# Gates of A and B, output projection and seven eighths of the up projection as seven products of halves of tokens, contraction and columns

## The chip, the cores and the metric

The kernel runs on one core of a Trainium2 chip. A core has a matrix engine (TensorE, PE in the profile; PEld is its weight loading), a vector engine (VectorE, DVE), a scalar engine (ScalarE, ACT), a general engine (GpSimd, POOL) and a queue engine (SyncE, SP) that issues transfers. The metric is the device time in microseconds. Three runs of the kernel before took 857.31, 858.68 and 859.06 us; the median is 858.68.

## The reference, cut to what matters

One encoder layer is applied to two groups of 256 tokens (512 in all) with shared weights, in float32.

```python
h = rms_norm(x, norm1_g)
proj = h @ w_in
qa, ka, va, qb, kb, vb, qm, ga, gb, gm = jnp.split(proj, ...)
...
merged = (jax.nn.sigmoid(ga) * (oa.reshape(B_, S, W_A) @ w_branch_a)
          + jax.nn.sigmoid(gb) * (ob.reshape(B_, S, W_B_OUT) @ w_branch_b)
          + jax.nn.sigmoid(gm) * (om.reshape(B_, S, W_M) @ w_branch_m))
x = x + merged @ w_out
h2 = rms_norm(x, norm2_g)
x = x + jnp.square(jax.nn.relu(h2 @ w_up)) @ w_down
...
return rms_norm(x, final_norm_g)
```

The model width is 1024 and the MLP's inner width 4096. Branch A is a windowed attention (512 channels out), B a dilated one (256), M a cross-attention to a memory (512).

## The kernel before

**Arithmetic.** Every float32 factor is split into a high half, rounded to the type that PE takes in one pass, and a low half, the rest. A product is three matmuls (`mm3`, lines 193 to 197): high by high, high by low, low by high. So each weight tile of 128 x 1024 numbers costs a load, a copy on ACT (high) and a subtraction on DVE or POOL (low): `halves` and `chunk`, lines 158 to 167. Two raw tiles and ten split tiles (five chunks) are there for weights.

**Layout.** Activations stand channels on partitions and tokens along the free dimension, eight tiles of 128 channels and 512 tokens. `fm` (line 199) makes one tile of 128 output channels and all 512 tokens from eight weight blocks of 128 x 128: 8 x 3 = 24 matmuls of 512 columns.

**Order.** The program is a list of units (`unit`, `run`, lines 145 to 191). `run` fetches and splits the weights of units ahead of the one that it emits; `ahead` says how many weight tiles (3 in the stages of this change). Everything on PE, DVE and ACT goes through `InOrder` (lines 62 to 74) and is executed in just this order by each engine; POOL's and SP's instructions are placed by the scheduler. What follows a product (reading its bank) is put on the list `later` and emitted with `flush` one unit on; the low halves of some weights and forms stand on the list `lows` and are emitted at the next unit.

**Stages.** Memory keys and values, projections and attention run to about 321 us. Then, for each of eight tiles of 128 output channels (`ff`), come a gate A and a gate B product (`gate`, line 764: 24 matmuls each) and `branches` (line 771: 12 for A, 6 for B, 12 for M), whose results are gated on DVE and summed on POOL; the gate of M was made before, between the attentions (`P_gm`). `merge` (line 791) splits the sums. `out_proj` (line 811) makes eight output channels tiles, adds x and splits the result with the second norm's gain (`H`). Last is the MLP in eight groups of 512 inner channels (line 1067): the up products of group c (`up`, four tiles in two halves each) alternate with the down products of group c-1. The down projection of groups 0 to 6 is already done as seven products of halves: `parts` (line 912) loads four blocks of the weight and makes their sums with accumulating transfers on POOL, `form` (line 931) makes sums of the activations on DVE, `product` (line 970) the matmuls, 512 columns each. The last group goes through `last_down` (line 1019).

Of the kernel before, what the change touches and what calls it, by code (L numbers as in the profile page):

```python
# [10 lines left out]
F32 = mybir.dt.float32  # L11
# [5 lines left out]
P = 128  # L17
# [60 lines left out]
def encoder_kernel(ctx: ExitStack, tc: tile.TileContext, a: dict, out: bass.AP):  # L78
# [32 lines left out]
    def f(x):  # L111
        return x.bitcast(F32)
# [34 lines left out]
    def unit(fn, *srcs):  # L147
        units.append((fn, srcs))
# [44 lines left out]
    def mm3(o, wh, wl, xh, xl, first, last, more=False):  # L193

        E.matmul(o, wh, xh, start=first, stop=False, skip_group_check=more)
        E.matmul(o, wh, xl, start=False, stop=False, skip_group_check=more)
        E.matmul(o, wl, xh, start=False, stop=last, skip_group_check=more)

    def fm(w, X, o):

        n = len(X)
        for k in range(n):
            c = slice(k * P, (k + 1) * P)
            mm3(o, w[0][:, c], w[1][:, c], X[k][:, 0], X[k][:, 1], k == 0, k == n - 1)
# [554 lines left out]
        unit(flush)  # L759


    MG, wb, sg = [], [], {}

    def gate(w, ff, br):
        p = bank()
        fm(w, X, p)
        g = h2("g")
        A.activation(g, p, AF.Sigmoid)
        sg[ff, br] = g

    def branches(w, *more):
        ff = len(MG)
        if more:
            wb[:] = more
        A.activation(GM[ff], GM[ff], AF.Sigmoid)
        sg[ff, 2] = GM[ff]
        c0 = (ff % 4) * 256
        parts = ((w[0][:, :512], w[1][:, :512], OA), (wb[0][0][:, c0:c0 + 256], wb[0][1][:, c0:c0 + 256], OB),
                 (w[0][:, 512:], w[1][:, 512:], OM))
        for br, (wh, wl, O) in enumerate(parts):  # L780
            p = bank()
            fm((wh, wl), O, p)
            V.tensor_tensor(sg[ff, br], p, sg[ff, br], op=ALU.mult)
        eng = V if ff == KD - 1 else G
        eng.tensor_tensor(sg[ff, 0], sg[ff, 0], sg[ff, 1], op=ALU.add)
        eng.tensor_tensor(sg[ff, 0], sg[ff, 0], sg[ff, 2], op=ALU.add)
        MG.append(sg[ff, 0])

    M = []

    def merge(*ks):
        for k in ks:
            x = s4("mg")
            A.activation(x[:, 0], MG[k], AF.Copy)
            (V, G)[k % 2 if k < KD - 1 else 0].tensor_tensor(x[:, 1], MG[k], f(x[:, 0]), op=ALU.subtract)
# [10 lines left out]
    unit(lambda: merge(KD - 1))  # L806


    X1, H = [], []

    def out_proj(w):
        ff = len(H)
        r = h2("xr")
        A.dma_start(r, a["xT"][:, ff])
        p = bank()
        fm(w, M, p)
        V.tensor_tensor(r, p, r, op=ALU.add)
        X1.append(r)
        x = s4("h")
        A.activation(x[:, 0], r, AF.Copy, scale=gains[:, 2, ff:ff + 1])  # L820
        V.scalar_tensor_tensor(x[:, 1], r, gains[:, 2, ff:ff + 1], f(x[:, 0]), op0=ALU.mult,
                               op1=ALU.subtract)
        H.append(x)

    for ff in range(KD):
        unit(out_proj, (a["w_o"][ff],))

# [14 lines left out]
    def mlp_pool():  # L842
        stages.close()
        at[0] = stages.enter_context(tc.tile_pool(name="ml", bufs=1))

    def block_tile():
        return at[0].tile([P, 1024], F32, tag="blk", name=nm("blk"), bufs=8)

    def turn_x1(t, hh):

# [20 lines left out]
    def up(w, ff, half):  # L871

        if half == 0:
            up_bank[ff] = w, bank()
        w, p = up_bank[ff]
        for k in range(4 * half, 4 * half + 4):
            c = slice(k * P, (k + 1) * P)
            mm3(p, w[0][:, c], w[1][:, c], H[k][:, 0], H[k][:, 1], k == 0, k == KD - 1)
        flush(9)
        if half:  # L880
            later.append(lambda: put_up(ff, p))
# [20 lines left out]
    def load_blocks(c):  # L902

        if c in blocks:
            return
        t = {n: block_tile() for n in "T2BC"}
        for n, b in (("T", "11"), ("2", "21"), ("C", "12"), ("B", "22")):
            SP.dma_start(t[n], block(c, b))
        G.dma_start(t["C"], block(c, "22"), accum_op=ALU.add)
        blocks[c] = t  # L910

    def parts(c, n):

        def go():
            load_blocks(c)
            hi, lo = w_tile(), w_tile()
            src = blocks[c][n[0]]
            A.activation(hi, src, AF.Copy)

            def low():  # L920
                V.tensor_tensor(lo, src, f(hi), op=ALU.subtract)
                if n[1:]:
                    G.dma_start(src, block(c, n[1:]), accum_op=ALU.add)  # L923

            lows.append(low)
            return hi, lo
        return go
# [3 lines left out]
    def form(c, name):  # L931

        lo, hi = UP[c, 0], UP[c, 1]
        A11, A21, A12, A22 = lo[:, :, :S], lo[:, :, S:], hi[:, :, :S], hi[:, :, S:]

        def less(u, v):
            d = h2("f").rearrange("p (j t) -> p j t", j=2)
            V.tensor_tensor(d, u, v, op=ALU.subtract)
            return d

        if name in ("P1", "P2", "Q4"):
            src = {"P1": A11, "P2": A12, "Q4": A22}[name]
        elif name == "Q5":
            src = forms[c, "S1"] = less(A21, A22)
        elif name == "Q6":
            src = forms[c, "S2"] = less(A11, forms.pop((c, "S1")))
        elif name == "P7":
            src = less(A11, A21)
        else:
            src = less(A12, forms.pop((c, "S2")))  # L950
# [8 lines left out]
    def add_to(k, i, p, op=ALU.add):  # L959
        if (k, i) in acc:  # L960
            V.tensor_tensor(acc[k, i], acc[k, i], p, op=op)
        else:
# [1 line left out]
            A.activation(acc[k, i], p, AF.Copy, scale=1.0 if op == ALU.add else -1.0)  # L964


    PRODUCTS = dict(P1=("T12", "a", "V", -1), P2=("2", "a", "11", 1), Q5=("T22", "d", "G", 1),
                    Q6=("T21", "c", "V", 1), P7=("C", "e", "G", -1), Q3=("B", "d", "12", 1), Q4=("T", "e", "21", 1))

    def product(w, c, name):  # L970
        _, bk, to, sign = PRODUCTS[name]
# [86 lines left out]
    unit(mlp_pool)  # L1058
    ORDER = ("P1", "P2", "Q5", "Q6", "P7", "Q3", "Q4")


    SUMMED = {1: ("12", "12"), 2: ("11", "11"), 3: ("21", "21"), 4: ("12", "V"), 5: ("21", "V", 1), 6: ("22", "G")}

    def make(c, n):
        unit(lambda: form(c, ORDER[n]))

    for c in range(NC):
        for h in range(8):
            ff, half = 4 * c + h // 2, h % 2
            unit(lambda *w, ff=ff, half=half: up(w[0] if w else None, ff, half), *([(a["w_up"][ff],)] if half == 0 else []))  # L1070
            if c == 0:
                unit(lambda h=h: turn_x1(h % 4, h // 4))
            if h == 1 and c < NC - 1:
                unit(lambda c=c: load_blocks(c))
            if h == 7 and c == NC - 2:
                unit(fetch_x1)
            if c == NC - 1 and h == 6:
                unit(lambda: ahead.__setitem__(0, 2))
            if c == NC - 1 and h in SUMMED:
                unit(lambda n=SUMMED[h]: later.append(lambda: combine(*n)))  # L1080
            if c and h < 7:
                for n in ((1, 2) if h == 0 else (h + 2,)):
                    if n < 7:
                        make(c - 1, n)
                unit(lambda w, c=c - 1, n=ORDER[h]: product(w, c, n), (parts(c - 1, PRODUCTS[ORDER[h]][0]),))
        if c == 0:
            unit(inv_ms)
            unit(lambda: ahead.__setitem__(0, 3))
        if c < NC - 1:
            make(c, 0)  # L1090
    unit(lambda *w: (kept.update({(0, 0): w[0], (1, 0): w[1]}), last_down(0, (0, 1))),
         *[(block(NC - 1, n),) for n in ("11", "21")])
    unit(lambda: later.append(lambda: combine("22", "V")))
# [84 lines left out]
```

## Time and profile before

| | |
|---|---|
| time, median of 3 runs | 858.68 us (857.31 to 859.06) |
| profiled execution | 859.08 us |
| its span, first to last instruction | 857.3 us |
| PE busy | 844.4 us (99%), 4080 matmuls |
| weight loads busy | 703.8 us (82%) |
| DVE busy | 462.8 us (54%) |
| ACT busy | 397.1 us (46%) |
| POOL busy | 216.0 us (25%) |
| read from memory | 101.93 MB |
| mean clock of PE granted | 0.993 |

The span is cut into 40 slices of 21.4 us on the page; a digit is the tenths of a slice in which an engine was busy. The groups of the page name an instruction by what it writes and reads: `ps<-x,w` is a product of normed activations and a weight, `ps<-mg,w` one of the output projection, `ps<-h,w` an up product, `ps<-w,f` a down product, `w<-raw,w` the low half of a weight, `f` a form, `acc` a sum of down products.

### The profile page before, as it was taken

Reading aid. Unit: us, or ns where it says so; the run is one execution under the profiler, and the core shown is the slowest. Engines: PE = TensorE matmul, PEld = TensorE weight load, DVE = VectorE, ACT = ScalarE, POOL = GpSimd, SP = SyncE. Lnnn points to the kernel's source line nnn. Section 1 sums busy time; section 2 is a strip of 40 time slices with the busy share of each in tenths; the row PEclk is TensorE's granted clock in tenths of the full one; section 3 lists DMA queues with packets and bytes.
Section 4 is the critical chain, followed back from the end, with each engine's and each line's share of the span. In section 5 each row is a group of like instructions: output and inputs, shape, how many; then the busy total and the mean of one; then the engine's idle time right before and its main releaser. Section 6 shows DMA issues by size and latency. Waiting matters only on the chain.

```text
span 857.3 us, 10785 instructions
## 1 busy us (share of the span) xinstructions
PE 844.4 (99%) x4080; PEld 703.8 (82%) x4080; DVE 462.8 (54%) x737; ACT 397.1 (46%) x690; POOL 216.0 (25%) x161
## 2 busy tenths in 40 slices
PE   9999999999999999999999999999999999999996
PEld 7788998888888888888888788888888888888885
DVE  6575535465452311423435542465767666767895
ACT  6455545565554333222323227564445353545453
POOL 2314554656556543211123000000000000000001
PEclk9999999999999999999999999999999999999998
DMA  8343122324241228432322445374747465645322
GB/s 284 115 119 109 62 99 86 98 63 115 85 119 64 75 74 286 132 99 86 110 99 74 147 147 161 110 204 107 205 109 208 111 185 121 178 120 172 75 75 98
DMA packets 47468, 106.87 MB, mean 125 GB/s; under 512 B 19358, under 2 KB 19604, under 8 KB 47416
## 3 DMA queue, kind: packets, MB, share of 16 engines
q1 hardware_dynamic: 39992, 85.69, 30.2%
q0 software_dynamic: 4256, 14.73, 9.7%
q10 hardware_dynamic: 3168, 5.77, 2.0%
q8 instruction: 32, 0.52, 0.3%
q14 instruction: 20, 0.16, 0.1%
HBM read 101.93 MB, written 4.24 MB: 124 GB/s over the span
## 4 chain that ended last, share of the span: by engine, by line
PE 84%; DVE 8%; ACT 5%; issue 2%; DMA 1%; POOL 0%; POOLq 0%; SPq 0%; DVEq 0%; ACTq 0%
PE ps L72 77%; PE sc L72 3%; PE o L72 2%; DVE w L72 2%; PE tp L72 2%; ACT w L72 2%; DVE f L72 1%; ACT sp L72 1%; DVE sp L72 1%; DMA mr<-in_memT 1%; ACT f L72 1%; DVE sq L72 0%; ACT r L72 0%; DVE mg L72 0%; DVE acc L72 0%
## 5 line engine op out<-in xcount | busy, mean ns | idle before, releaser
L72 PE MATMUL ps<-x,w 128*128 128x512 f32 x1080 | 252.5, 391 | 0.0
L72 PEld LDWEIGHTS ps<-x,w 128*128 128x128 f32 x1080 | 201.0, 188 | 41.3
L72 PE MATMUL ps<-h,w 128*128 128x512 f32 x768 | 184.5, 391 | 0.0
L72 PEld LDWEIGHTS ps<-h,w 128*128 128x128 f32 x768 | 143.7, 188 | 29.5
L72 PE MATMUL ps<-w,f 128*128 128x512 f32 (+1 forms) x696 | 164.1, 387 | 1.3 <-DVE acc L72 1.0
L72 DVE TENSOR_TENSOR w<-raw,w 128x1024 fp32r<-128x1024 f32 (+1 forms) x79 | 96.4, 1223 | 115.3 <-ACT w L72 115.2
L72 PEld LDWEIGHTS ps<-w,f 128*128 128x128 f32 x696 | 128.7, 188 | 29.9 <-issue 3.4
L72 ACT ACTIVATE w<-raw 128x1024 fp32r<-128x1024 f32 (+2 forms) x116 | 119.7, 1036 | 21.9 <-DMA raw<-in_w_mem 7.5
L161 POOL TENSOR_TENSOR w<-raw,w 128x1024 fp32r<-128x1024 f32 (+1 forms) x37 | 87.3, 2361 | 120.1 <-ACT w L72 94.9
L72 DVE TENSOR_TENSOR w<-blk,w 128x1024 fp32r<-128x1024 f32 x49 | 59.5, 1224 | 47.7 <-ACT w L72 47.6
L923 POOL DMA_DIRECT2D blk<-in_w_dn x21 | 18.1, 864 | 240.2 <-DVE w L72 240.2
L72 ACT ACTIVATE w<-blk 128x1024 fp32r<-128x1024 f32 x49 | 50.7, 1047 | 15.4 <-DMA blk<-in_w_dn 15.4
L72 DVE TENSOR_TENSOR acc<-acc,ps 128x512 f32<-128x512 f32 x82 | 52.9, 682 | 2.9 <-PE ps L72 2.9
L72 ACT ACTIVATE f<-f 128x512 fp32r<-128x512 f32 x28 | 17.7, 633 | 75.4 <-DVE f L72 75.4
L72 ACT ACTIVATE sp<-sp,st 128x256 f32<-128x256 f32 (+1 forms) x48 | 25.8, 538 | 57.7 <-DVE st L72 57.7
L72 ACT ACTIVATE g<-ps 128x512 f32<-128x512 f32 x16 | 9.6, 598 | 88.4 <-PE ps L72 88.4
L72 DVE TENSOR_TENSOR sum<-o,lo 64x256 f32<-64x256 f32 x24 | 10.0, 417 | 66.5 <-ACT lo L72 66.3
L72 PE MATMUL ps<-mg,w 128*128 128x512 f32 x192 | 44.2, 391 | 1.5 <-ACT mg L72 0.9
L72 PEld LDWEIGHTS ps<-mg,w 128*128 128x128 f32 x192 | 36.0, 188 | 9.6 <-ACT mg L72 1.3
L72 ACT ACTIVATE r<-ps 128x512 f32<-128x512 f32 x32 | 18.9, 591 | 50.7 <-PE ps L72 50.7
L72 PE MATMUL ps<-w,x 128*128 128x384 f32 (+1 forms) x192 | 39.9, 363 | 0.0
L469 POOL TENSOR_TENSOR sp<-sp,st 128x512 f32<-128x512 f32 (+1 forms) x32 | 36.7, 1147 | 6.5 <-DVE st L72 3.6
(146 smaller groups left out, 959.2 us busy)
## 6 DMA issues: line engine op xcount, KB each, us to landing
raw<-in_w_up SPq DMA_DIRECT2D x32, 512.0 KB, 4.7
blk<-in_w_dn SPq DMA_DIRECT2D x28, 512.0 KB, 6.7
blk<-in_w_dn POOLq DMA_DIRECT2D x28, 512.0 KB, 5.7
raw<-in_w_g SPq DMA_DIRECT2D x24, 512.0 KB, 3.3
raw<-in_w_b SPq DMA_DIRECT2D x12, 512.0 KB, 3.3
raw<-in_w_bam SPq DMA_DIRECT2D x8, 512.0 KB, 3.3
raw<-in_w_o SPq DMA_DIRECT2D x8, 512.0 KB, 3.2
raw<-in_w_mem SPq DMA_DIRECT2D x7, 512.0 KB, 3.3
```

What stands on the lines that cost most here:

```text
L72: return self.tc.keep_in_program_order(method(*args, **kw))
L161: sub[0].tensor_tensor(lo[:, c], raw[:, c], f(hi[:, c]), op=ALU.subtract)
L469: G.tensor_tensor(s[:, :, :w], s[:, :, :w], st[:, 6:8].unsqueeze(2).to_broadcast([P, 2, w]), op=ALU.mult)
L923: G.dma_start(src, block(c, n[1:]), accum_op=ALU.add)
```

## The change

The gates of A and B, the output projection and the up projection of groups 1 to 7 are made as seven products of halves. A group is 512 output channels; tokens, contraction and output channels are halved, which gives four blocks of activations (512 contraction channels x 256 tokens), four of weights and four of results (256 channels x 256 tokens).

- `halves_of` makes the sums of the activations' blocks once for a stage, in eight pieces: S1 (pieces 0, 1; the form of Q5), S2 (2, 3; Q6), S4 (4, 5; Q3) and S3 (6, 7; P7, written over the second half of the first four tiles). Each ends with a high half on ACT and a low half on DVE.
- `seven` makes the products in the order P1, P2, Q5, Q3, Q6, P7, Q4. A product is 24 matmuls of 256 columns in one bank. Its weights stand in two tiles: T (block 11, to which an accumulating transfer of POOL adds 12, 22 and 21 after the splits of P1, Q5 and Q6) and C (12 and 22); two more come raw. Each product has one 128 x 1024 split on ACT and DVE. `take` reads the banks: two copies on ACT and one read in place, and five operations of DVE a group.
- Gates: two halves of the channels (q) and two branches alternate. The branch M products (`memory_branch`) move ahead of all gates, with one piece of the forms after each; A and B (`branches`) follow each q. Their gating and sums are all on DVE now, by halves of the tokens.
- Output projection: two groups alternate, with a piece of M's forms after each of the first eight products. `put` adds x and splits H by quarters of 256 tokens.
- Up: group 0 stays as it was, with another order of the contraction and six pieces of H's forms beside it. Groups 1 to 7 alternate a product of `up_seven` with a down product. The down products come in the same new order (Q3 before Q6), and their blocks 21 and 22 come through the raw tiles.

On DVE, the output projection before, where a result tile `xr` follows the product `ps` and is split into `h`, with one weight `w` to split between two of them:

```order
L72 TENSOR_TENSOR xr_4075<-ps_4077,xr_4075 128x512
L72 SCALAR_TENSOR_TENSOR h_4103<-xr_4075,gains,h_4103 128x512
L72 TENSOR_TENSOR w_4108<-raw_4106,w_4107 128x1024
L72 TENSOR_TENSOR xr_4112<-ps_4114,xr_4112 128x512
L72 SCALAR_TENSOR_TENSOR h_4140<-xr_4112,gains,h_4140 128x512
L72 TENSOR_TENSOR w_4145<-raw_4143,w_4144 128x1024
```

and on DVE in the changed program, between the weights of the products Q3 of the two groups (`w_4805`, `w_4851`) and with the form that these read (`f_4635` its high half, `f_4636` its low half):

```order
L72 TENSOR_TENSOR w_4805<-raw_4806,w_4804 128x1024
L72 TENSOR_TENSOR d_4810<-mg_4499,d_4725 128x256
L72 TENSOR_TENSOR d_4810<-d_4810,mg_4499 128x256
L72 TENSOR_TENSOR d_4810<-mg_4502,d_4725 128x256
L72 TENSOR_TENSOR d_4810<-d_4810,mg_4502 128x256
L72 TENSOR_TENSOR f_4634<-d_4810,f_4633 128x512
L72 TENSOR_TENSOR xr_4645<-ps_4693,xr_4645 128x256
L72 SCALAR_TENSOR_TENSOR h_4842<-xr_4645,gains,h_4842 128x256
L72 TENSOR_TENSOR xr_4647<-ps_4693,xr_4647 128x256
L72 SCALAR_TENSOR_TENSOR h_4846<-xr_4647,gains,h_4846 128x256
L72 TENSOR_TENSOR w_4851<-raw_4852,w_4850 128x1024
L72 TENSOR_TENSOR d_4856<-mg_4581,d_4765 128x256
```

Where one tile of 512 columns and its split stood between two weights, a piece of the forms and four operations on quarters stand now.

At the start of the gate stage, DVE in the changed program takes the first memory product (`ps_3172`, gated in place in `q_2700`), the weight of the fifth memory product (`w_3217`), the second piece of X's forms and the next memory product:

```order
L72 TENSOR_TENSOR f_3156<-d_3191,f_3155 128x512
L72 TENSOR_TENSOR q_2700<-ps_3172,q_2700 128x512
L72 TENSOR_TENSOR w_3217<-raw_3215,w_3216 128x512
L72 TENSOR_TENSOR d_3222<-x_462,x_514 128x512
L72 TENSOR_TENSOR d_3221<-d_3222 128x256
L72 TENSOR_TENSOR d_3225<-x_466,x_517 128x512
L72 TENSOR_TENSOR d_3221<-d_3225 128x256
L72 TENSOR_TENSOR f_3156<-d_3221,f_3155 128x512
L72 TENSOR_TENSOR q_2782<-ps_3201,q_2782 128x512
```

Before, DVE had at this place only the low halves of the gates' weights and the multiplies of the three branches; all rows of `d` and `f` are new.

On POOL in an MLP group of the changed program, the accumulating transfers into C of the next down and up group (`blk_6450`, `blk_6572`) stand ahead of the first ones into T of this group (`blk_6161`, `blk_6039`):

```order
L861 DMA blk_5747<-in_w_up 128x2x512
L1136 DMA blk_5609<-in_w_dn 128x1024
L1118 DMA blk_6450<-in_w_dn 128x1024
L847 DMA blk_6572<-in_w_up 128x2x512
L861 DMA blk_6161<-in_w_up 128x2x512
L1136 DMA blk_6039<-in_w_dn 128x1024
```

Before, POOL had four such transfers a group, one into C and three into T, all of the down projection.

The core of the diff:

```diff
+    SEVEN = ("P1", "P2", "Q5", "Q3", "Q6", "P7", "Q4")
+    ONTO = dict(P1="12", Q5="22", Q6="21")
+    def halves_of(X, forms):
...
+        def put(S, j, d):
+            hi, lo = (x[:, 512 * j:512 * j + 512].rearrange("p (j t) -> p j t", j=2) for x in forms[S])
+            A.activation(hi, d, AF.Copy)
+            V.tensor_tensor(lo, d, f(hi), op=ALU.subtract)
+
+        def less(x, y, out):
+
+            e = pair()
+            V.tensor_tensor(e, f(x), f(y), op=ALU.subtract)
+            V.tensor_tensor(out, e[:, 0], e[:, 1], op=ALU.add)
+
+        def minus(x, d, out):
+            V.tensor_tensor(out, f(x[:, 0]), d, op=ALU.subtract)
+            V.tensor_tensor(out, out, f(x[:, 1]), op=ALU.add)
...
+        def go(n, w):
...
+            for j in range(2):
+                for k in range(4):
+                    c = slice(j * 512 + k * P, j * 512 + (k + 1) * P)
+                    xh, xl = form_of(X, forms, n, k)
+                    mm3(b[:, j * S:(j + 1) * S], w[0][:, c], w[1][:, c], xh, xl, new and j == k == 0, k == 3, j > 0 or not new)
+            flush(9)
+            later.append(lambda: take(n, b))
...
     for ff in range(KD):
-        for br in range(2):
-            unit(lambda w, ff=ff, br=br: gate(w, ff, br), (a["w_g"][ff, br],))
-        if ff == KD - 1:
-            unit(lambda: merge(*range(KD - 1)))
-        unit(branches, (a["w_bam"][ff],), *([(a["w_bb"][ff // 4],)] if ff % 4 == 0 else []))
+        unit(memory_branch, (lambda ff=ff: half_chunk(a["w_bam"][ff][:, 512:]),))
+        unit(pieces[ff])
+    for q in range(2):
+        for n in range(7):
+            for br in range(2):
+                unit(g4[q, br][1][n][0], g4[q, br][1][n][1])
...
-    for ff in range(KD):
-        unit(out_proj, (a["w_o"][ff],))
...
+                r, x, g = X1[ff][:, t], H[ff], gains[:, 2, ff:ff + 1]
+                V.tensor_tensor(r, y[:, j * S:(j + 1) * S], r, op=ALU.add)
+                A.activation(x[:, 0, t], r, AF.Copy, scale=g)
+                V.scalar_tensor_tensor(x[:, 1, t], r, g, f(x[:, 0, t]), op0=ALU.mult, op1=ALU.subtract)
...
+    for n in range(7):
+        for q in range(2):
+            unit(*o7[q][1][n])
+            if n < 4:
+                unit(pieces_o[2 * n + q]) if n + q else None
...
     for c in range(NC):
-        for h in range(8):
-            ff, half = 4 * c + h // 2, h % 2
-            unit(lambda *w, ff=ff, half=half: up(w[0] if w else None, ff, half), *([(a["w_up"][ff],)] if half == 0 else []))
...
+        for n in range(7 if c else 0):
+            unit(*u7[c][1][n])
...
+            down_unit(c - 1, n)
```

More of the change, by code (lines that the diff above doesn't have):

```diff
@@ L759, in encoder_kernel, with late_pool, block_tile @@
         unit(flush)
-    MG, wb, sg = [], [], {}
-    def gate(w, ff, br):
-        p = bank()
[L766 to L772, printed above, removed]
+    def late_pool():
+        stages.close()
+        at[0] = stages.enter_context(tc.tile_pool(name="ml", bufs=1))
+    def block_tile():
+        return at[0].tile([P, 1024], F32, tag="blk", name=nm("blk"), bufs=8)
+    SEVEN = ("P1", "P2", "Q5", "Q3", "Q6", "P7", "Q4")
@@ L789, in encoder_kernel, with gated @@
+    def gated(ff, br, p):
+        for i in range(2):
+            c, x = slice(i * S, (i + 1) * S), sg[ff, br, i]
+            V.tensor_tensor(x, p[:, c], x, op=ALU.mult)
+            V.tensor_tensor(MG[ff][:, c], MG[ff][:, c], x, op=ALU.add)
     M = []
@@ L806, in encoder_kernel @@
-    unit(lambda: merge(KD - 1))
-    X1, H = [], []
[L811 to L823, printed above, removed]
@@ L825, in encoder_kernel, with half_chunk @@
-    for ff in range(KD):
-        unit(out_proj, (a["w_o"][ff],))
+    def half_chunk(src):
+        raw, hi, lo = raw_tile(), w_tile(), w_tile()
+        SP.dma_start(raw[:, :512], src)
+        A.activation(hi[:, :512], raw[:, :512], AF.Copy)
+        lows.append(lambda: V.tensor_tensor(lo[:, :512], raw[:, :512], f(hi[:, :512]), op=ALU.subtract))
+        return hi[:, :512], lo[:, :512]
+    unit(start_late)
+    pieces = halves_of(X, XF)
+    g4 = {(q, br): gates(q, br) for q in range(2) for br in range(2)}
@@ L835, in encoder_kernel @@
+    unit(start_out)
+    pieces_o = halves_of(M, MF)
+    o7 = [out_seven(q) for q in range(2)]
+    unit(lambda: pieces_o[0]())
+    for n in range(7):
[3 more added lines that the diff above has]
+                unit(pieces_o[2 * n + q]) if n + q else None
+    unit(lambda: flush(9))
     NC = 8
@@ L875, in up @@
         w, p = up_bank[ff]
-        for k in range(4 * half, 4 * half + 4):
+        order = (2, 3, 6, 7, 0, 1, 4, 5)
+        for k in order[4 * half:4 * half + 4]:
             c = slice(k * P, (k + 1) * P)
-            mm3(p, w[0][:, c], w[1][:, c], H[k][:, 0], H[k][:, 1], k == 0, k == KD - 1)
+            mm3(p, w[0][:, c], w[1][:, c], H[k][:, 0], H[k][:, 1], k == order[0], k == order[-1])
         flush(9)
@@ L916, in go @@
             hi, lo = w_tile(), w_tile()
-            src = blocks[c][n[0]]
+            if n in ("21", "22"):
+                src = raw_tile()
+                SP.dma_start(src, block(c, n))
+            else:
+                src = blocks[c][n[0]]
             A.activation(hi, src, AF.Copy)
@@ new lines, in make, with down_unit @@
+    def make(c, n):
+        unit(lambda: form(c, SEVEN[n]))
+    def down_unit(c, n):
+        for m in ((1, 2) if n == 0 else (n + 2,)):
+            if m < 7:
+                make(c, m)
+        unit(lambda w: product(w, c, SEVEN[n]), (parts(c, PRODUCTS[SEVEN[n]][0]),))
+    pieces_up = halves_of(H, HF)
+    for h in range(8):
+        ff, half = ((0, 0), (1, 0), (0, 1), (1, 1), (2, 0), (2, 1), (3, 0), (3, 1))[h]
+        unit(lambda *w, ff=ff, half=half: up(w[0] if w else None, ff, half), *([(a["w_up"][ff],)] if half == 0 else []))
+        unit(lambda h=h: turn_x1(h % 4, h // 4))
+        if h == 0:
+            unit(start_up)
+        if h < 6:
+            unit(pieces_up[h])
+        if h == 1:
+            unit(lambda: load_blocks(0))
+        if h == 0:
+            u7[1] = up_seven(1)
+            unit(u7[1][0])
@@ L1078, in encoder_kernel @@
                 unit(lambda: ahead.__setitem__(0, 2))
[L1079 to L1085, printed above, removed]
+            if c == NC - 1 and n in SUMMED:
+                unit(lambda n=SUMMED[n]: later.append(lambda: combine(*n)))
```

236 lines of the change are left out of this document (201 added, 35 removed).

## The prediction

> **What bounds the kernel now.** I read the page's busy shares and 40 slices first, then PE's own timeline for the stages, then the windows, then VectorE's (DVE's) timeline for its prices.
>
> ```profile
> PE 844.4 (99%) x4080; PEld 703.8 (82%) x4080; DVE 462.8 (54%) x737; ACT 397.1 (46%) x690; POOL 216.0 (25%) x161
> PE   9999999999999999999999999999999999999996
> DVE  6575535465452311423435542465767666767895
> PE 84%; DVE 8%; ACT 5%; issue 2%; DMA 1%; POOL 0%; POOLq 0%; SPq 0%; DVEq 0%; ACTq 0%
> ```
>
> PE has work in every slice, and 84% of the chain of waits is PE's. DVE works half the time, but six to seven tenths in the MLP slices. So the kernel lasts as long as its matmuls, and a change pays by taking columns off PE only while DVE, which splits every weight and form into halves, keeps ahead.
>
> ```profile
> 320.83 16.52 PE L72 MATMUL ps<-x,w 128*128 128x512 f32 x72
> 337.19 2.88 PE L72 MATMUL ps<-oa,w 128*128 128x512 f32 x12
> ...
> 467.75 4.92 PE L72 MATMUL ps<-mg,w 128*128 128x512 f32 x21
> 473.56 0.49 PE L72 MATMUL ps<-mg,w 128*128 128x512 f32 x1 [0.89 <-ACT mg L72]
> ...
> 513.30 2.89 PE L72 MATMUL ps<-h,w 128*128 128x512 f32 x12
> 516.03 0.60 PE L72 MATMUL tp<-ident,xr 128*128 128x128 f32 x4
> 516.38 3.02 PE L72 MATMUL ps<-h,w 128*128 128x512 f32 x12
> 519.24 0.60 PE L72 MATMUL tp<-ident,xr 128*128 128x128 f32 x4
> 519.59 2.99 PE L72 MATMUL ps<-h,w 128*128 128x512 f32 x12
> ...
> 541.59 2.88 PE L72 MATMUL ps<-w,f 128*128 128x512 f32 x12
> ...
> 846.79 2.92 PE L72 MATMUL ps<-w,f 128*128 128x256 f32 x23
> ```
>
> These are runs of equal matmuls (start, length). A run's length holds the last one's latency, so the pace comes from neighbouring starts: (337.19-320.83)/72 = 0.227 us for a matmul of 512 columns. For 256 columns, all in one run: 2.92 less the 0.28 that one takes, over 22, is **0.120 us**. That is more than half of 0.227, so seven products of halves cost 168 x 0.120 = 20.2 us where 96 whole matmuls cost 21.8: a group saves **1.6 us**, 7%, and not an eighth.
>
> The Trainium skill, "TensorE: Matmul & The Clock Gate", section Back-to-back issue gap, gives N/2.4 + 2.5 ns, by which a group would save 20.7 - 18.3 = 2.4 us (an estimate from that page). The trace's 0.227 and 0.120 both lie above it and decide here; by the page the total below would fall by 8 us, to 871.
>
> **The change part by part.** *Matmuls.* Thirteen groups (4 gates, 2 output projection, 7 up) turn 1248 matmuls of 512 columns into 2184 of 256: 282.9 - 262.1 = **-20.8 us**. The gate stage alone falls by 6.4.
>
> *The merge wait.* Before, the output projection takes 513.30 - 467.75 = 45.6 us for 192 x 0.227 = 43.6, the difference being the waits for mg of its last channel. Its place is now inside the stretch costed below: **-2.0**.
>
> *What DVE pays.* Each product needs its own split weight, each sum and difference is DVE's, and the forms are split once more.
>
> ```profile
> 615.39 2.36 DVE L72 TENSOR_TENSOR w<-blk,w 128x1024 fp32r<-128x1024 f32 x2
> 607.51 1.28 DVE L72 TENSOR_TENSOR acc<-acc,ps 128x512 f32<-128x512 f32 x2
> 92.83 0.42 DVE L72 TENSOR_TENSOR om<-o,om 128x256 fp32r<-128x256 f32 x1 [0.50 <-ACT om L72]
> 93.17 0.16 DVE L72 RECIPROCAL st<-st 128x2 f32<-128x2 f32 x1
> 590.48 0.69 DVE L72 TENSOR_TENSOR f<-f,f 128x512 fp32r<-128x512 f32 x1 [0.70 <-ACT f L72]
> 482.34 0.75 DVE L72 SCALAR_TENSOR_TENSOR h<-xr,gains,h 128x512 fp32r<-128x512 f32 x1 [0.79 <-ACT h L72]
> L72 ACT ACTIVATE om<-o 128x256 fp32r<-128x256 f32 x8 | 3.1, 383 | 6.5 <-PE o L72 6.4
> ```
>
> From start to start DVE spends 2.36 - 1.22 = 1.14 us on 1024 columns, 0.60 on 512 and 0.34 on 256 (93.17 - 92.83); 0.06 more for a scalar_tensor_tensor; about 0.09 more where the next one needs its result. Where the high half must come back from ScalarE (ACT) before DVE can go on, the f and h rows show 0.70 and 0.79 us of idle DVE. I price such a round trip at 0.75 for 512 columns; for 256 at 0.55, from ACT's 383 ns and the two handovers. All DVE work keeps the program's order, so such a wait stops every split behind it, and PE waits for those.
>
> *Memory branches and gates.* PE reaches the first memory product at 320.83 + 24 x 0.227 = 326.3 and finishes the eighth, unhindered, at 348.0. DVE reaches the multiply of the first one's result when it lands, at 329.2, and behind it stand, in order, seven more multiplies (0.60), the splits for memory products 4 to 7 (0.60), pieces 1 to 7 of the forms (one of 3.4 us, four of 2.8, two of 3.8, round trips included) and four gate weights (1.14). Added up in that order the weights of the four first gate products are ready at 347.6, 352.2, 357.7 and 363.3; PE would want the fourth at 348.0 + 3 x 2.88 = 356.7. **+6.6**; 0 if no round trip shows, 12 if ACT is busy when asked. After that DVE has 14 products' time for 14 weights and ten sums, and is ahead again.
>
> *Output projection to the first down product.* This decides. Gates and branches now end at 326.3 + 21.8 + 80.6 + 32.6 + 6.6 = 467.9; the last branch unit starts at 463.8. In the four branch units DVE has 15.5 us of rows from 454.4 on (the multiply of the first product, when that lands); so it takes up the last unit's multiplies at 469.9, 3.2 us late. From there to the split of the first down form, in order, stand 19 weights (21.7), 38 operations of 512 columns (22.8), 72 of 256 (24.5) and 16 scalar_tensor_tensor of 256 (6.4), with the 0.3 of inv_ms 75.7 us; 12 round trips of 512 (9.0) and 20 of 256 (11.0), and some 3 for dependent neighbours: 98.5 in all. The first down product then starts at 469.9 + 98.5 = 568.4. PE alone would be there at 467.9 + 14 x 2.88 + 8 x 3.2 (half an up column and its transposes, by the rows above) + 2.88 = 536.7. **+31.7**. Its first half shows at Q3, whose form stands behind four pieces and the first 11-blocks' put: PE is through Q5 at about 490 and gets Q3's form at about 506. The bounds: with DVE in time and every round trip free, 466.7 + 75.7 = 542.4, +5.7; with half of the 32 round trips also behind one of ACT's weight copies (about 0.95 each), +47. I take the sum as it stands, since every idle f and h row of the trace shows the round trip.
>
> *The up and down groups.*
>
> ```profile
> 588.00:629.00 41.00, 40.83 (x181) 33.52 (x180) 28.23 (x36) 19.34 (x26) 3.45 (x4) 1.00 0.58 154
> 794.00:857.00 63.00, 55.54 (x256) 46.04 (x254) 49.01 (x75) 28.07 (x48) 4.33 (x6) 0.96 0.29 84
> q1 hardware_dynamic: 39992, 85.69, 30.2%
> q0 software_dynamic: 4256, 14.73, 9.7%
> blk<-in_w_dn POOLq DMA_DIRECT2D x28, 512.0 KB, 5.7
> 588.28 0.86 POOL L923 DMA_DIRECT2D blk<-in_w_dn  x1 [12.04 <-DVE w L72]
> ```
>
> In the windows the columns are busy time of PE, its weight loads, DVE, ACT and POOL, then clock, DMA share and GB/s. A whole group takes PE 84 x 0.227 + 168 x 0.120 = 39.2 us now; DVE has 14 weights, 30 operations of 512 and three round trips: 16.0 + 18.0 + 2.1 = 36. So DVE nearly fills the group but PE ends it. The first one (with the last forms and what DVE still owes) gives **+1.0**. DMA: 28 accumulating loads take 9.7% of the span, 3.0 us of all engines each; a plain 512 KB takes 0.302 x 857/163 = 1.6. A group had 8 plain and 4 accumulating, 24 us (0.58 of 41, as the window says); now 8 and 8, 36 of 39. POOL's queue holds the next group's two C loads ahead of this group's first T load, which Q5 waits for. Issue, landing, high and low half take 0.9 + 5.7 + 1.05 + 1.2 = 9 us of the 11.2 between P1 and Q5, and the splits run some 6 us ahead of PE, so I take **+2.0** over all groups; 0 to 18 (3 us of late landing in each of six).
>
> *The end.* In the last group DVE has thirteen scaled sums more and the last form's splits; added up, the last up weight comes 0.7 and the second kept weight 1.4 us after PE wants it: **+2.2**, 0 to 5.
>
> Sum: -20.8 - 2.0 + 6.6 + 31.7 + 1.0 + 2.0 + 2.2 = +20.7. The profiled execution took 859.08 us (span 857.3 and 1.8 around it), so 879.8; it lies 0.4 above the median of the runs, so **879.5 us**.
>
> **The rivals.** *DVE keeps up.* Round trips hidden and no late start leave 5.7 of the stretch and nothing before it: -20.8 - 2.0 + 5.7 = -17, **842 us**, faster. It decides if DVE's rows from the last branch on cost under some 78 us rather than 98. For it: DVE is only 54% busy, and splits are asked for three products ahead. Against: 75.7 us of pure work stand there beside 70 of PE, and both round trips are rows of the trace. A middle, with half of the waits hidden, ends at 856 to 864.
>
> *Accumulating loads bind.* If each group waits 3 us for T, +16 more: **896**. For it: 36 of 39 us of DMA. Against: the lead of 6 us.
>
> *Weight loads bind.* PEld's share rises with 936 more loads; at 0.130 a matmul, +22: **901**. The run of 23 at 0.120 had a load for each and speaks against it.
>
> That the change doesn't do what it says is excluded by the built order: 2184 matmuls of 256 columns stand for the 1248.
>
> **How the numbers follow.** Forecast, DVE binding from the last branch to the first down product, 864 to 893: 0.73. DVE keeps up: 0.09. The middle: 0.07, of which 0.04 lies within 0.2% of before (about what a measurement of this kernel tells from no change) and 0.02 below. Loads: 0.08. Weight loads: 0.03. The page's pace would give 871, inside the forecast. Faster 0.11, same 0.04, slower 0.85. The range, 860 to 896, leaves out the first rival, half the middle and the far loads.
>
> **What would show it.** Right: runs of 256-column matmuls at 0.120; in the output projection a hole of some 16 us in PE before Q3, ended by DVE or ACT f; the first down product near 568 instead of 541.59; groups of 39 to 41 us after it; DVE busy above 70% and PE below 96%. Wrong: no PE gap over 3 us there (first rival), or ACT w waiting long for DMA blk in each group (second), or a pace above 0.125 (third). My largest doubt is how much of the 23 us of round trips and dependences DVE really idles.

## The result, and the profile after

The changed kernel takes **966.53 us** (median of 4 runs, 963.65 to 968.79) against 858.21 us for the kernel before beside it (4 runs, 857.31 to 859.06): **1.126 times as long**, 95% interval 1.122 to 1.130. The forecast was 879.5 us with a range of 860 to 896: slower, as measured, but by 21 us and not by 108.

Busy shares, three rows of slices and the chain of waits on the page of the changed kernel:

```profile
PE 854.8 (89%) x5016; PEld 748.0 (78%) x5016; DVE 627.2 (65%) x1047; ACT 475.0 (49%) x818; POOL 245.1 (25%) x193
PE   9999999999999977999964596699998989798976
DVE  6585354655432485685876776667687777786985
PEclk9999999999999997999977798799999999999999
PE 39%; DVE 32%; ACT 17%; issue 10%; DMA 1%; ACTq 0%; POOL 0%; POOLq 0%; DVEq 0%
```

PE's share of the chain falls from 84% to 39%, DVE's and ACT's rise to 49% together; yet DVE is busy only 65% and ACT 49%. So neither is simply full. PE's timeline shows where PE stands still (start, length, what it did, and in brackets the idle time ahead and what ended it):

```profile
492.68 8.80 PE L72 MATMUL ps<-mg,w 128*128 128x256 f32 x48 [8.30 <-ACT e L72]
518.03 1.68 PE L72 MATMUL ps<-f,w 128*128 128x256 f32 x6 [10.89 <-ACT e L72]
551.03 8.49 PE L72 MATMUL ps<-mg,w 128*128 128x256 f32 x48 [10.12 <-DVE e L72]
598.25 5.53 PE L72 MATMUL ps<-w,f 128*128 128x512 f32 x12 [8.75 <-ACT f L72]
609.88 3.04 PE L72 MATMUL ps<-f,w 128*128 128x256 f32 x24
637.08 3.04 PE L72 MATMUL ps<-h,w 128*128 128x256 f32 x24
750.23 4.62 PE L72 MATMUL ps<-h,w 128*128 128x256 f32 x24 [2.13 <-ACT e L72]
781.29 3.10 PE L72 MATMUL ps<-h,w 128*128 128x256 f32 x24 [1.21 <-DVE e L72]
```

The first three waits are in the output projection, the fourth is the first down product (598.25; forecast 568.4), the last two come back in every MLP group. Five of them name `e`: PE must not add the second product of a pair (P2, Q3, Q4) to a bank before ACT or DVE has read the first one out of it (P1, Q5, P7). ACT makes three such copies in a group, of P1, Q5 and Q3, and not two as said under "The change". I had PE wait only for weights and forms. That reading, a shared bank, was my first suspicion.

The windows and DVE's list of waits say something else. Windows of the first gates, of the stretch from the output projection to the first down product, and of six MLP groups (from P7 to P7; columns as in the prediction: PE, its weight loads, DVE, ACT, POOL):

```profile
350.10:404.90 54.80, 44.68 (x337) 43.90 (x338) 34.49 (x45) 24.22 (x34) 9.68 (x8) 0.88 0.63 138
478.50:598.20 119.70, 78.33 (x489) 70.99 (x487) 85.75 (x153) 50.99 (x90) 12.34 (x11) 0.83 0.64 163
637.10:914.30 277.20, 247.47 (x1514) 218.88 (x1513) 210.45 (x267) 143.50 (x195) 48.54 (x46) 0.98 0.76 178
```

DVE's waits in the second and then in the third of these windows, and ACT's in the third (total us, times, longest):

```profile
DVE w L72 <- ACT w L72: 11.5, 18, 1.4
DVE h L72 <- ACT h L72: 9.2, 16, 0.6
DVE f L72 <- ACT f L72: 8.9, 12, 1.2
DVE mg L72 <- ACT mg L72: 1.9, 4, 0.5
DVE rr L72 <- ACT junk L72: 0.9, 1, 0.9
```

```profile
DVE w L72 <- ACT w L72: 53.9, 36, 2.3
DVE f L72 <- ACT f L72: 12.6, 18, 0.7
```

```profile
ACT f L72 <- DVE f L72: 68.2, 18, 5.9
ACT e L72 <- DVE e L72: 59.7, 17, 4.1
ACT w L72 <- DMA blk<-in_w_dn: 1.8, 3, 1.0
ACT e L72 <- PE ps L72: 0.5, 2, 0.2
```

In the groups DVE's work and its waits for ACT make 210.45 + 53.9 + 12.6 = 276.95 of 277.2 us; in the stretch ahead 85.75 + 32.4 = 118.2 of 119.7. DVE has no wait for PE or a transfer in either list, and in the groups ACT waits 128 us for DVE but 0.5 for PE. In these two stretches next to nobody waits for PE any more: DVE and ACT pass the work back and forth, and PE follows. How, two timelines of one group show, DVE's and then ACT's:

```profile
773.99 1.29 DVE L72 TENSOR_TENSOR e<-e,e 128x512 f32<-128x512 f32 x2
776.99 1.23 DVE L72 TENSOR_TENSOR w<-blk,w 128x1024 fp32r<-128x1024 f32 x1 [1.70 <-ACT w L72]
...
780.47 0.68 DVE L72 TENSOR_TENSOR e<-e,ps 128x512 f32<-128x512 f32 x1
783.46 1.23 DVE L72 TENSOR_TENSOR w<-blk,w 128x1024 fp32r<-128x1024 f32 x1 [2.31 <-ACT w L72]
```

```profile
781.18 0.63 ACT L72 ACTIVATE e<-e 128x512 f32<-128x512 f32 x1 [3.27 <-DVE e L72]
781.84 0.63 ACT L72 ACTIVATE u<-e 128x512 f32<-128x512 f32 x1
782.38 1.99 ACT L72 ACTIVATE w<-blk 128x1024 fp32r<-128x1024 f32 x2
```

DVE finishes `e` at 781.15. Only then ACT, whose next instruction in order is the put of that result, can go on: relu, square, and behind them the copies of weights for products to come, which need nothing of that result. DVE's next instruction is the low half of the first of these, so it idles 2.31 us: ACT's 0.63 and 0.63, and about 1.0 for one of the two copies.

### The profile page after: what moved, and what is told of

The parts are those of the page before. It is cut to its first block, busy times and chain, and to the rows that moved or that the text cites. A ratio compares the mean times of both kernels' runs of the same rounds, so it can differ in the third digit from the quotient of the medians.

```text
span 963.1 us, 13281 instructions
## 1 busy us (share of the span) xinstructions
PE 854.8 (89%) x5016; PEld 748.0 (78%) x5016; DVE 627.2 (65%) x1047; ACT 475.0 (49%) x818; POOL 245.1 (25%) x193
## 4 chain that ended last, share of the span: by engine, by line
PE 39%; DVE 32%; ACT 17%; issue 10%; DMA 1%; ACTq 0%; POOL 0%; POOLq 0%; DVEq 0%
PE ps L72 32%; DVE w L72 10%; ACT w L72 8%; DVE acc L72 5%; DVE d L72 4%; DVE f L72 4%; DVE e L72 4%; ACT e L72 3%; PE sc L72 2%; PE o L72 2%; ACT f L72 2%; PE tp L72 1%; DVE q L72 1%; DVE blk L72 1%; ACT h L72 1%
## 5 line engine op out<-in xcount | busy, mean ns | idle before, releaser
L72 PE MATMUL ps<-x,w 128*128 128x512 f32 (+1 forms) x1080 | 215.9, 358 | 11.9 <-ACT e L72 8.3
L72 PE MATMUL ps<-w,f 128*128 128x512 f32 (+1 forms) x696 | 170.9, 396 | 19.5 <-DVE acc L72 10.5
L72 PE MATMUL ps<-f,w 128*128 128x256 f32 x936 | 120.2, 288 | 21.9 <-ACT e L72 19.0
L72 PE MATMUL ps<-h,w 128*128 128x256 f32 (+1 forms) x768 | 116.0, 308 | 25.7 <-DVE e L72 12.8
L72 PEld LDWEIGHTS ps<-f,w 128*128 128x128 f32 x936 | 118.3, 196 | 24.9 <-ACT e L72 19.9
L72 PEld LDWEIGHTS ps<-h,w 128*128 128x128 f32 x768 | 105.0, 200 | 37.4 <-issue 15.6
L72 DVE TENSOR_TENSOR w<-blk,w 128x1024 fp32r<-128x1024 f32 x75 | 91.7, 1222 | 44.0 <-ACT w L72 44.0
L861 POOL DMA_DIRECT2D blk<-in_w_up x21 | 27.9, 1328 | 197.6 <-DVE w L72 187.0
L72 ACT ACTIVATE w<-blk 128x1024 fp32r<-128x1024 f32 x75 | 76.0, 1048 | 1.9 <-DMA blk<-in_w_dn 1.8
L72 ACT ACTIVATE f<-f 128x512 fp32r<-128x512 f32 x28 | 17.6, 627 | 73.9 <-DVE f L72 73.9
L72 PE MATMUL ps<-mg,w 128*128 128x256 f32 x192 | 29.1, 320 | 18.4 <-DVE e L72 10.1
L72 DVE TENSOR_TENSOR w<-wb,w 128x1024 fp32r<-128x1024 f32 x25 | 30.6, 1224 | 19.4 <-ACT w L72 19.4
```

Of the source, the lines that this page charges most:

```text
L72: return self.tc.keep_in_program_order(method(*args, **kw))
L861: G.dma_start(by2(src), block(ONTO[n]), accum_op=ALU.add)
```

## The experiments

**Theory A**: this loop sets the time; a stage lasts as long as DVE's work and its waits for ACT together. **Theory B**: the read between two products of one bank holds PE. All runs below are single ones, beside runs of the kernel before of 857.0 to 859.2 us; and most differences that are read from them are of 5 us and more. The four runs of the changed kernel itself lie 5.1 us apart, and eight runs whose programs are the same up to the first memory product (e1, e3, e5, e6, e8, e12, e15, e18) reach it anywhere from 324.0 to 326.4 us; so a difference under some 5 us in the whole time is a hint only, and a stage is better compared by its length. A group is the mean of six: the distance of the first P7 (`ps<-h,w` behind `ps<-f,w`) in PE's timeline from the last one, over 6.

| run | us | first down product | first and last P7 | group |
|---|---|---|---|---|
| changed kernel | 966.5 | 598.25 | 637.08, 914.28 | 46.2 |
| e1 own banks | 970.0 | 593.96 | 632.11, 919.35 | 47.9 |
| e2 copy first | 929.5 | 589.00 | 626.37, 879.92 | 42.3 |
| e5 puts later | 937.8 | 593.16 | 631.42, 892.93 | 43.6 |
| e3 plain out | 929.7 | 564.22 | 602.78, 880.50 | 46.3 |
| e4 plain out, copy first | 898.3 | 555.47 | 592.82, 850.36 | 42.9 |
| e6 plain out, puts later | 909.7 | 562.68 | 601.82, 864.84 | 43.8 |
| e7 e6, forms later | 905.2 | 560.39 | 598.79, 860.79 | 43.7 |
| e8 e6, own banks | 900.6 | 555.58 | 592.38, 857.37 | 44.2 |
| e9 e7, C later | 902.2 | 557.96 | 596.06, 857.88 | 43.6 |
| e13 e9, order held | 910.0 | 558.69 | 597.25, 860.22 | 43.8 |
| e15 order held, alone | 986.3 | 600.47 | 639.34, 936.68 | 49.6 |
| e17 e7, no sums | 879.1 | 558.01 | 596.42, 834.71 | 39.7 |
| e18 no sums alone | 965.0 | 599.59 | 638.58, 915.75 | 46.2 |

**Own banks (e1).**

```diff
-            if new:
-                banks[BANK[n]] = bank()
+            banks[BANK[n]] = bank()
...
-                    mm3(..., xh, xl, new and j == k == 0, k == 3, j > 0 or not new)
+                    mm3(..., xh, xl, j == k == 0, k == 3, j > 0)
```

> In every product of seven the second of a pair (P2, Q3, Q4) opens a bank of its own, so PE need not wait until the first's sum has been read; nothing is added on any engine. It leaves out the first product's share of that sum (P1 in 11, Q5 in 12, P7 in 21). Theory A (DVE and ACT, each in order, wait for each other's results, and a stage lasts as long as DVE's work and its waits for ACT together: 34.9 + 9.2 + 2.1 = 46.2 of a group's 46.3 us): PE's waits for e go and come back at w and f; a group still takes 46 us, the whole 950 to 968. Theory B (the read between two products of one bank holds PE, whose waits for e by ACT and DVE are 48.0 + 24.2 us): a group takes 40 to 42, the whole 890 to 905.

970.04 us, just above what Theory A allows and far from Theory B; groups take 47.9 us, and not 40 to 42. PE's waits in the groups of that run (671 to 920 us), and DVE's beside them:

```profile
PE ps L72 <- DVE acc L72: 32.3, 14, 3.5
```

```profile
DVE w L72 <- ACT w L72: 53.6, 34, 2.4
```

PE waits no longer for `e`, but for the next thing that DVE is late with. Theory B falls as the cause in the groups; why a group is even 1.7 us longer here stays open.

In the first gates it does not fall. There the same run takes 49.4 us (351.05 to 400.46) where the changed kernel takes 54.8, and no wait of PE is longer than 2.1 us, where one of 8.3 for `e` stood:

```profile
351.05:400.46 49.41, 43.40 (x336) 41.96 (x337) 32.84 (x44) 24.04 (x34) 9.69 (x8) 0.97 0.70 155
```

**The weight copy ahead of the puts (e2), or the puts one product later (e5).** Both leave the work as it is and open the loop; e2 in `run`, e5 in `take`.

```diff
                 if fetch:
                     lower()
+                if fetch != early[0]:
                     fn(*got[i])
```

```diff
-                put("22", e["22"])
+                later.append(lambda: put("22", e["22"]))
```

> From the gates on, the copy of the weight three products ahead stands in ACT's queue before the reads and puts of the products done, where it stood behind them; the work is the same. Theory A: DVE no longer waits for a weight's high half behind a put that waits for DVE; of its 9.2 us of waits for w in a group 1 to 2 are left, a group takes 39 to 41 us, the gates of the first half 41 to 46 instead of 54.8, the whole 885 to 905. Theory B: ACT's reads of P1 and Q5 come 1.05 us later, so PE waits longer at P2 and Q3: 966 to 985.

> The weight copies stay where the change put them; instead the puts that need a result of DVE (12, 22 and 21) are put into ACT's queue one product later, when DVE has long written it. Theory A as the runs so far leave it (DVE and ACT hold each other up; where the copies were moved ahead, ACT waited 4 us in each group for a T block of the accumulating loads instead): of DVE's 9.2 us of waits for w in a group 2 to 3 are left and no wait of ACT for T comes in, a group takes 39.5 to 42 us, the whole 905 to 935. Should the group stay above 44, the puts were not what held the copies up.

929.45 and 937.8 us: the loop is worth 29 to 37 us by its order alone, which is what Theory A says and Theory B denies. DVE's waits for `w` in the six groups fall from 53.9 us to 17.6 in e2 and 37.1 in e5. But e2 wins half of what I expected and e5 falls just short; groups stay at 42.3 and 43.6 us, and 2.9 and 6.2 us of these waits are left in each, where 1 to 2 and 2 to 3 were expected. The first gates, for which e2 promised 41 to 46 us, take 54.0 in e2 and 53.8 in e5: there the loop's order wins 1 us and banks of their own 5. ACT's waits in the groups of e5 show a new line of some 4 us a group:

```profile
ACT w L72 <- DMA blk<-in_w_dn: 26.7, 5, 6.6
```

**The output projection as before (e3), and with either of those (e4, e6).** The eight `out_proj` units of before, 16 split weights and eight pieces of forms less.

> The output projection as before (192 matmuls of 512 columns, no forms, 16 splits less), all else as changed. Both theories: the 80.9 us of that stage become 45 to 48 (43.6 of matmuls and the merge's wait), the first up part 28 to 39, a group stays at 46.3, the whole 922 to 935. By my forecast, which charged that stage and the up part together some 31.7 us, it would be 966 less 32 = 934; above 945 neither.

> The weight copies first in ACT's queue, and the output projection as before. Theory A: the two gains add up, since they fall in different stages: groups of 39 to 41 us, the stage of the output projection 45 to 48, the whole 850 to 872, so near the time before the change. Theory B: the gain of the plain output projection alone: 922 to 940.

> The puts one product later, and the output projection as before. The two gains add up: some 37 us below the run with the puts alone, 868 to 898. With groups of 39.5 us and the first gates and the first up group unchanged (13 and 12 us lost) it would be 870.

929.72, 898.33 and 909.67 us. The output projection by halves costs 37 us with its forms, as expected; with the copies first it adds to nearly the same (31), with later puts 28. The expected 850 to 872 and 868 to 898 were missed, since the groups stay above 42 us.

**What is left in the relaxed kernel (e7, e8).** e7 takes the low half of a down product's form one product later (`later` in place of `lows`) and moves the memory branches' low halves to POOL; e8 is e6 with e1's banks.

> As the run with later puts and plain output projection, with two waits or loads less for DVE: the low half of a down product's form is taken one product later, so that DVE need not wait 0.7 us for ACT's high half (2.1 us a group), and the low halves of the eight memory branch weights go to POOL (4.8 us less for DVE before the first gates). Theory A: 5 to 15 us below that run where its groups are still over 39.5 us; the hole at the first gates (8.7 us) shrinks to 4 to 6.

> As the run with later puts and plain output projection, with a bank of its own for P2, Q3 and Q4 (the first product's share of 11, 12 and 21 left out). Now DVE and ACT are less tightly coupled, so this prices the read of the shared bank itself: Theory A: within 6 us of that run. Theory B for what is left: faster by what PE still waits there for e, 10 to 25 us.

905.17 us: 4.5 less, just short of the expected 5 to 15, groups unmoved; the hole at the first gates was 7.0 us instead of 8.3 in e6, but e9 and e13, with the same gates, have 8.2 and 6.7. And 900.61, 9 less than e6, between the two expectations: 2.3 of it already lies ahead of the first memory product, where the two programs are the same, 4.8 in the first gates (49.4 us instead of 54.2), and the rest in the first group and the end, while the six groups take 44.2. So once the loop is opened the shared bank costs some 5 us in the first gates, perhaps 4 in the first group and the end, and nothing in the groups.

**The accumulating loads.** The new wait of ACT is for a T block. In e7 the T load of a down product left POOL 0.7 us behind the next up group's load of C and landed 10.1 us after its issue. e9, and e12 on the changed kernel, emit the C loads later; e10 is e9 with gates and branches as before, e11 e9 with own banks.

```diff
+        def load_c():
             G.dma_start(by2(t["C"]), block("22"), accum_op=ALU.add)
...
+            if n == 1 and c > 1:
+                unit(u7[c][3])
```

> As the run with later puts, later low halves of forms and plain output projection, whose groups still take 44 us; there ACT waits 5.5 to 7.2 us in each group for a T block, whose accumulating load stands in POOL's queue behind the next group's accumulating load of C and lands 10.1 us after its issue instead of 5 to 6. Here the accumulating loads of C are issued one and a half groups' steps later, behind the T loads of Q5. If that queue is the second bound, ACT's wait for T shrinks to 2 us or less, a group takes 39.5 to 41.5 us, the whole 880 to 893. If it is not, groups stay at 44 and the whole at 900 to 908.

> The changed kernel with the later C loads and nothing else. Theory A: the handovers between DVE and ACT set the group, and this load is hidden behind them: a group stays at 46 us, the whole 958 to 972. If the loads bind by themselves: groups of 42 to 44, the whole 945 to 955.

> As the run with the C loads later, and the gates and branches as before too, so that of the change only the seven products of the up groups are left. The gates lose their 6.4 us of fewer columns and win back what PE loses from 340 to 375 us (some 13 us): 5 to 10 us below that run, 868 to 888. With groups of 39.4 us and nothing lost elsewhere it would come to 850; the first up group, which still waits for the forms, speaks against that.

> As the run with the C loads later, with a bank of its own for P2, Q3 and Q4 (the first product's share of 11, 12 and 21 left out). With the handovers and the queue relaxed, what PE still waits for e is the price of the shared bank: 5 to 12 us below that run, most of it at the first gates and the first up group, if theory B holds for the rest; within 4 us of it if DVE and ACT set those places too.

902.23, 965.14, 892.91 and 898.27 us. The first two do not test the queue: POOL's instructions are placed by the scheduler, and POOL's timeline of e9 has the up group's C load (L850) still straight ahead of the T load (L1114):

```profile
694.92 1.20 POOL L850 DMA_DIRECT2D blk<-in_w_up  x1 [3.42 <-DMA blk<-in_w_up]
695.63 1.42 POOL L1114 DMA_DIRECT2D blk<-in_w_dn  x1
```

e10 wins 9.3 us, within its 5 to 10, though not the level it named; e11 wins 4.0, with first gates of 49.4 us instead of 54.2. Next the loads were held to the written order (`InOrder` for POOL's accumulating loads), in e13 on e9, in e14 with plain gates, in e15 on the changed kernel; e16 is e14 with two pieces of the up forms made during the output projection.

> The run with later C loads left the up group's C load where it was: POOL still issued it straight before the down product's first T load, 0.7 us apart, so the queue was not tested. Here POOL's accumulating loads are held to the written order (T for Q5 of up and down, T for Q3's successor, then C). If the queue is the second bound behind the handovers: the T load of the down product lands 6 to 7 us after its issue instead of 10.5, ACT's wait for it (6.1 us a group) falls below 2, a group takes 39.5 to 41.5 us instead of 44.4, the whole 878 to 892. If not: 898 to 905.

> The changed kernel with only the later C loads, now in POOL's real order. Theory A: the queue is hidden behind the handovers between DVE and ACT, a group stays at 46 us, the whole 958 to 970. If the queue binds by itself: groups of 42 to 44, 940 to 955.

> As the run before it, with the gates and branches as before the change. The same gain of the queue, from 893: 868 to 882; without it 889 to 896.

> As the run with plain gates and C loads later in the queue, with two of the eight pieces of the up forms made while the output projection still runs, where DVE is busy only 25 of 45 us. The first up group, at whose Q3 PE waits 8 us, gets 6 us of DVE's time back: 5 to 9 us below that run, 860 to 876; no change if that wait is not DVE's load.

909.98, 986.3, 895.12 and 893.17 us. The groups take 43.7 to 49.6 us and not 39.5 to 41.5, so the gain of the queue did not come: e13 and e15 lie above both of their ranges, e14 in the one without that gain, and e16 is not told from e14. In e13 the down T load for Q5 lands 6 to 7 us after its issue, as meant, but now the C load of the down product is late: issued at 714.39 behind an up T load, it lands after 8.7 us, and ACT waits 4.7 for it. PE's hole moves from Q3 to Q4, and ACT's wait for blocks of the down weight in the six groups is 24.3 us, where e7 has 30.1. In e15 groups grow to 49.6 us: this order of these loads costs even behind the loop. In e16 PE's wait at the first up group's Q3 stays at 8.3 us, so the room that DVE got earlier does not reach it.

So the sums were taken out: in e17 from e7, in e18 from the changed kernel.

```diff
-            G.dma_start(by2(t["C"]), block("22"), accum_op=ALU.add)
+            if c_sum:
+                G.dma_start(by2(t["C"]), block("22"), accum_op=ALU.add)
...
-                if n in ONTO:
+                if n in ONTO and c_sum:
```

> As the run with later puts, later low halves of forms and plain output projection (groups of 44.1 us, 905), but the up and down groups have no accumulating loads at all: the weights of Q5, Q6 and Q4 are made from block 11 alone and those of P7 from block 12 alone, so the sums are left out; every split, copy and matmul stays. If the queue of accumulating loads is what holds the relaxed groups: no wait of ACT for a block, DVE's wait for w in a group falls from 7.7 to 3 us or less, a group takes 39.4 to 41, the whole 870 to 888. If groups stay above 43, the handovers that are left (forms, e after DVE) hold them.

> The changed kernel without the accumulating loads of the up and down groups (the same sums left out), nothing else. Theory A: the handovers alone hold the group, 45 to 46.5 us, the whole 955 to 968, since ACT waits for a block only 0.7 us in three groups there. If loads and handovers share it: 42 to 44, 935 to 950.

879.11 and 964.99 us, both as expected. DVE's waits in the six groups of e18 are those of the changed kernel to the tenth:

```profile
DVE w L72 <- ACT w L72: 53.9, 36, 2.3
DVE f L72 <- ACT f L72: 12.6, 18, 0.7
```

The same list of e7 and of e17, and a window of one group of e17:

```profile
DVE w L72 <- ACT w L72: 41.0, 24, 5.8
```

```profile
DVE w L72 <- ACT w L72: 17.8, 19, 1.9
```

```profile
675.50:714.90 39.40, 39.40 (x253) 35.82 (x252) 34.78 (x45) 23.61 (x32) 0.00 (x0) 1.00 0.32 108
```

Four cells: with the loop, 46.2 us a group with the loads and 46.2 without; with the loop opened, 43.7 with and 39.7 without, of which the middle groups take 39.40, all of it PE. The loop is the bound of the changed kernel's groups; the accumulating loads stand right behind it, and PE behind both. Whether the loads hold the opened group by their order in POOL's queue or by their number these runs don't tell, since e9 and e13 moved the wait and did not take it away. The lowest time of a kernel with all its sums is 892.9 us, so none of these versions beats the kernel before.

## Why the prediction was wrong

The forecast span was 879.8 - 1.8 = 878.0 us, that of the profiled execution 963.1: 85.1 us. By its own steps:

| step | forecast | measured | error |
|---|---|---|---|
| gates and branches end at | 467.9 | 478.5 | +10.6 |
| from there to the first down product | 100.5 | 119.8 | +19.3 |
| six groups | 6 x 39.2 | 6 x 46.2 | +42 |
| the first up and down group and the end | 74.4 | 87.7 | +13 |

**Matmuls: right.** The run at 609.88 gives (3.04 - 0.28)/23 = 0.120 us for 256 columns, with a load for each. The weight-load rival is out. The Trainium skill, "TensorE: Matmul & The Clock Gate", section Back-to-back issue gap, gives the formula of the prediction as the gap of single matmuls, without a weight load for each; by it the pace would be 0.109, and the trace does not agree. (Over thirteen groups that pace would have taken some 10 us off the sum, and not 8.)

**"So DVE nearly fills the group but PE ends it": the step that failed.** DVE's work was nearly right (16.0 + 18.0 = 34.0 forecast, 210.45/6 = 35.1 measured), and so were the round trips (2.1, and 12.6/6 = 2.1); what was left out is DVE's wait for weights' high halves, 53.9/6 = 9.0 us a group. I had priced a round trip only for forms and `h`, and took the weights as ready since they are asked for three products ahead. They are asked for, but their copy on ACT stands behind a put that waits for DVE. The kernel before shows that already. DVE's waits, and then ACT's, in its MLP from 560 to 800 us:

```profile
DVE w L72 <- ACT w L72: 53.0, 34, 4.0
DVE f L72 <- ACT f L72: 19.5, 25, 2.6
```

```profile
ACT f L72 <- DVE f L72: 63.2, 23, 3.3
ACT r L72 <- PE ps L72: 44.8, 12, 6.3
```

That is 12.4 us of DVE's waits in 41, so with 28.2 busy its group was already accounted for to 40.6 of 41.0. It cost nothing, since ACT itself waited for PE there, 7.7 us a group; in the changed kernel's groups that wait is 0.1 us, so I read it as the slack that the change used up. The forecast's 36 with the 9.0 measured in the changed kernel gives 45, within some 1 us of the 46.2. That these waits hold the groups e2 and e5 show, by taking some of them away, and e18, which takes the loads away and leaves these waits and the group as they were.

**"Output projection to the first down product", +31.7: the right place and mechanism, too small.** I added up DVE's work and 23 us of round trips and dependences, 98.5 us from the last unit's multiplies at 469.9. They began at 481.5, 1 us later behind the end of the branches than forecast, and from there to the first down product passed 116.7 us. DVE's work was 82.9 of them, where 75.7 and 3 for dependences were forecast, and its waits 32.4, where 20.0 were: 20.9 of them are the round trips and the other 11.5 again the wait for weights. My upper bound named that case, half of the round trips behind a weight copy, and I left it out of the sum; with +51 (119.8 less the 68.8 of PE alone) the stage came out even above this bound of +47. The hole at Q3 was forecast as one of 16 us; it came as three, 8.3 at P2, 10.9 at Q3 and 10.1 at Q4, at the second products of the shared banks, which I had not seen. From the output projection's start to the first down product e1 takes 120.8 us and the changed kernel 119.8, so there the bank decides only where the loss is seen. That the output projection by halves costs 37 us e3 shows.

**"Memory branches and gates", +6.6: too small by 10.6.** In the first gates DVE was busy 34.49 us and waited 20.1 for ACT, together 54.6 of 54.8. DVE's waits, and then those of ACT for PE:

```profile
DVE w L72 <- ACT w L72: 17.5, 15, 3.3
DVE x L72 <- ACT x L72: 1.9, 4, 0.5
DVE f L72 <- ACT f L72: 0.7, 1, 0.7
```

```profile
ACT e L72 <- PE ps L72: 5.1, 4, 1.3
ACT g L72 <- PE ps L72: 4.3, 2, 2.9
```

I took the multiplies and pieces with their round trips, no wait for weights, and no read between P1 and P2. The sum of DVE's work and waits is filled here too, but ACT also waits 9.4 us for PE, so PE stands in this loop with the other two, and the shared bank is part of it: e2 and e5, which open the loop between DVE and ACT, leave a hole of 8.7 and 8.3 us at P2, while banks of their own win 4.8 to 5.3 us of the stage in e1, e8 and e11. What the rest of its loss needs to go was not found.

**The first group and the end: +1.0 and +2.2 became some 16** (the +2.0 for loads is in the 74.4). 8.1 of it is the wait for `e` at the first group's Q3, with slow matmuls behind it. e16 did not move it. With banks of their own (e1, e8, e11) it is gone, but a wait of 3.4 to 4.9 us for `acc` and smaller ones for weights come in its place, and the group is only 0.7 to 2.3 us shorter; what holds it stays open.

**The rivals.** DVE keeping up is refuted. Accumulating loads binding is not what happened (e18), but it was the next thing in line: once the loop is opened they hold a group at 43.7 us (e7 against e17), near the 39.2 + 3 that this rival charged. DVE busy above 70%, my sign for the forecast, did not come (65%): waits in a loop are not busy time.

## What to carry to other kernels

Where engines run in program order, an engine's share of a stage is its busy time plus its waits for an engine that waits for it in turn; when these fill the stage and no one waits for PE, the pair is the bound, here at 76% and 52% busy. Before adding work to such an engine, look for who still waits for the engine that is to be relieved: that wait is the slack there is. A read or put that needs a fresh result belongs behind the copies that other engines ask for next, and a wait that PE names (here the shared bank) may be only the last link: take it away in an experiment, stage by stage, before building on it. Here the bank was worth nothing in the groups and 5 us in the first gates.

## What the runs showed of the hardware

PE's clock fell after holes. The twelve matmuls of 512 columns behind the 8.75 us wait at 598.25 took 5.53 us, where undisturbed runs of twelve take 2.91; the granted clock in that stretch was 0.59:

```profile
592.00:603.50 11.50, 5.25 (x12) 3.64 (x12) 6.43 (x14) 8.63 (x17) 0.00 (x0) 0.59 0.51 157
```

A hole of 2.13 us can be enough: the 24 matmuls behind it at 750.23 took 4.62 us instead of 3.04, at a granted clock of 0.72 from 749 to 755. It need not: behind a hole of 2.50 us in e7, at 629.56, such a run took 3.13. I had not charged this; what it costs by itself was not tested.

In the six groups of the changed kernel accumulating loads of 512 KB on POOL's queue landed 5.3 to 7.2 us after their issue where none was issued within 2 us ahead of them; three issued within 1.6 us (693.19, 693.91 and 694.78) landed after 5.8, 8.3 and 10.5 us, that is, at 698.98, 702.16 and 705.31, some 3.2 us apart.
